# Weight sums by DMA, last state columns split, and two zeroed banks for lags in an S5 mixer kernel

## The chip, the cores and the metric

The kernel runs on one core of a Trainium2 chip. The core has five engines that work side by side, each on its own queue of instructions in order: PE (TensorE, matmuls; its weight loads are shown as PEld), DVE (VectorE), ACT (ScalarE), POOL (GpSimd) and SP (SyncE, here used for DMA). They meet through semaphores: an instruction waits until a semaphore has a count, and whatever stands behind it on the same engine waits too. Times are device microseconds (us), smaller is better.

## What is computed

One layer of a diffusion backbone over 1024 latent tokens of width 1024, with a prefix of 256 context tokens. The layer is an S5 mixer (a bidirectional state space model with complex diagonal states, 64 groups of 16 channels and 64 states) with GELU and a gate (GLU), then a SwiGLU FFN, each behind an RMSNorm with shift, scale and gate. Cut to what matters here:

```python
def s5_direction(u_ctx, u_lat, lam_re, lam_im, log_step, b_re, b_im, c_re, c_im):
    lam_bar = jnp.exp(lam * jnp.exp(log_step)[:, None])
    b_bar = ((lam_bar - 1.0) / lam)[..., None] * lax.complex(b_re, b_im)
    def run(u, h0):
        bu = jnp.einsum('lgh,gnh->lgn', u, b_bar)
        bu = bu.at[0].add(lam_bar * h0)
        _, h = lax.associative_scan(_linear_combine, (a, bu), axis=0)
        return jnp.einsum('lgn,ghn->lgh', h, c_mat).real, h[-1]
...
x = x + m_l[2][:, None] * y_l
h_l = modulate(rms_norm(x, norm_ffn[i]), m_l[3][:, None], m_l[4][:, None])
x = x + m_l[5][:, None] * swiglu(h_l, ffn_w1[i], ffn_w3[i], ffn_w2[i])
return rms_norm(x, norm_final)
```

## The kernel before

Eight tokens are taken as one chunk, so the latent stream is 128 chunks. Inside a chunk the output comes from a lag matrix (what the 8 tokens of the chunk give to each other) and from the state at the chunk's border. The 64 groups are handled as 8 units `k` of 8 groups; a quarter `q` holds two units.

Up to some 129 us the kernel loads, builds powers of lambda, projects the tokens into the states and runs the context. Then three things stand beside each other:

- `scan()` on DVE: the recurrence over the latent chunks. At each step it makes two products in `st1` and `st2`, which are the columns 384 to 512 of two PSUM banks, `LTb` (`ltb` in the profile) and `ltc`, and adds them to the states. For two of the quarters it fills all columns itself; for the others it goes in steps of two, and POOL restores the columns between. `scan()` is recorded ahead of the order string below, so its instructions are known to the program when the string's are added.
- `PROG1`, an order string written by hand: each word is an operation that is recorded at its place on all engines that it uses.
- After it the PSUM pools of this stage are closed, and `PROG2`, a second order string, follows: the late halves, the gelu, the transposes and the GLU. Then come the gates and the FFN.

The words that matter: `A` ada matmuls (modulation) with their weight loads on SP. `B0` turns the input matrices on PE and copies them on ACT. `Cqp` builds part p of the weights CL of quarter q: two products on POOL (`prod`), the second into a buffer `ct`, and their sum, whose way is a letter of `HOWS`: P is on PE (matmuls with an identity into a bank, L672, and ACT copies, L673), E is an add on POOL (L77), Y is a DMA issued by POOL that accumulates (L675). `Gq` is a sign change of the loaded C matrices on ACT (L655), which `Lq` loads. `Kn` computes lag rows (`k_mats`, PE L809 to L817), from two PSUM tiles that ACT zeroes ahead (L771), copies them on ACT (L821) and stores them to HBM (L822). `Tn` loads them back as lag matrices (SP, L830). `F` restores columns of the scan on POOL. `Rk`, `Zk`, `zk` copy the states in turned order for the backward direction (L902 on ACT, L904 elsewhere). `Pk` is the lag matmuls (`x_mm`, L945) and the early states (L922) of unit k into banks of the stage's PSUM pool, `Yn` ACT's copy of them out (L993). `Nk` is the late states, `Dk` their add on DVE, `Hk` the gelu. `Qk` is lag matmuls and all states in one (L935), only for units 6 and 7. `M0` and `M1` make modulation columns.

A PSUM pool of this stage has three banks `pw` in turn, and one `pm`. A helper `tt` records every two-operand op, so these have line 77. In the profile `c` stands for a weight tile, `ra`, `rw`, `rxa`, `rxc`, `ru` for regions of SBUF.

Of the kernel before, what the change touches and what calls it, by code (L numbers as in the profile page):

```python
# [17 lines left out]
P = 128  # L18
# [5 lines left out]
T = 8  # L24
G = 64
HC = 16
NS = 64
EPS = 1e-6
MAGIC = 12582912.0
HOWS = "PPPP PPEE PEEE EEEE"  # L30
ZEN = "VVSVSVSV"
PROG1 = ("A22 B0 A26 C02 G1 A30 A34 C03 A40 K0 A44 A48 C10 K1 L2 A54 G2 C11 A60 F10 C12 F11 C13 T0 T1 T2 T3 A64 M0 M1 K2 R0 P0 Y0 Y1 K3 L3 R1 C20 P1 Y2 Y3 T4 T5 G3 T6 T7 C21 C22 C23 K4 R2 P2 Y4 Y5 K5 R3 P3 Y6 Y7 T8 T9 T10 T11 C30 C31 R4 P4 Y8 Y9 C32 C33 R5 P5 Y10 Y11 K7 K6 M2 m0 F30 F31")
PROG2 = ("T12 T13 T14 T15 Z0 N0 Z1 Z2 D0 Z3 N1 D1 Z4 H0 H1 N2 D2 H2 w0 w1 l1 N3 Z5 D3 H3 N4 D4 z6 z7 I0 J0 I1 J1 H4 N5 D5 I2 J2 H5 I3 J3 W0 W1 x0 x1 x2 x3"
         " Q6 H6 I4 J4 Q7 b0 I5 J5 H7 g03 g13 I6 J6 g23 g05 g15 I7 J7 V1 w20 w21 g26 x10 x11 x12 x13")
LOG2E = 1.4426950408889634
LN2H = 0.693359375
LN2L = -2.12194440e-4
# [5 lines left out]
def s5_ffn_kernel(tc, a, out):  # L43
# [3 lines left out]
    with ctx:  # L47
# [611 lines left out]
        def cl_ops(q, part, ct, how):  # L659
# [7 lines left out]
            def add():  # L667
# [8 lines left out]
                else:  # L676
# [14 lines left out]
                 7: [(1, [0], 0, 8)], 8: [(1, [0], 8, 16)], 9: [(1, [1, 2, 3])],  # L691
                 11: [(2, [0], 0, 8)], 12: [(2, [0], 8, 16)], 13: [(2, [1, 2, 3])],
                 14: [(3, range(4), 0, 8)]}
        ct_ = [view(r, kb, [8, T, HC]) for r, kb in ((RW, 0), (RC[3], 0), (RC[3], 4), (RA, STB))]
        cts = [[ct_[0], ct_[0], ct_[1], ct_[2]], [ct_[0], ct_[1], ct_[2], ct_[0]], [ct_[1], ct_[2], ct_[0], ct_[1]], [ct_[3], ct_[0]] * 2]
        CL0 = cl_ops(0, 0, cts[0][0], SY) + cl_ops(0, 1, cts[0][1], SY)
        CLAT = {12: 1, 13: 1, 14: 2}
        for hb in range(16):
# [164 lines left out]
            while rest:  # L863
                one()

        def fill(q, h, reg, kb):

            tmps = [view(reg, kb + i, [256]) for i in range(2)]
            st, c0 = STQ[q], 32 * h
            for e in (0, 8):  # L870
                rot(st[:, 32 + c0:63 + c0:2, :, e:e + 8], st[:, 31 + c0:62 + c0:2, :, e:e + 8], LS[:, 0], 16 * q + e, E, tmps)

        MBd = dr.tile([2, 2, 512], F32, tag="mbd", name="mbd")

# [34 lines left out]
        def yview(k, gp):  # L909
            return Y[:, k].rearrange("p t (a e h) -> p e a t h", e=2, h=HC)[:, gp]  # L910

        def states_mm(k, pts, half, hs, start):

            for a_ in range(4):
                for ri in range(2):
                    for d in range(2):
                        cs_ = slice(64 * (half ^ d), 64 * (half ^ d) + 64)
                        c0 = 31 + 64 * half
                        for gp in range(2):
                            ps = slice(64 * gp, 64 * gp + 64)  # L920
                            st = hs[ps, :, ri, a_] if d else STQ[k // 2][ps, c0:c0 + 64, ri, 8 * (k % 2) + a_]
                            PE.matmul(flat(pts[gp][cs_, a_]), st, flat(CL[k // 2][ps, ri, d, 4 * (k % 2) + a_]),  # L922
                                      start=start and ri == 0, stop=ri == 1 and (start or a_ == 3))

        def states_all(k, pts, hs):

            for a_ in range(4):
                for ri in range(2):
                    for d in range(2):
                        for c in range(2):  # L930
                            cs_ = slice(64 * c, 64 * c + 64)
                            for gp in range(2):
                                ps = slice(64 * gp, 64 * gp + 64)
                                st = hs[ps, cs_, ri, a_] if d else STQ[k // 2][ps, 31 + 64 * c:95 + 64 * c, ri, 8 * (k % 2) + a_]
                                PE.matmul(flat(pts[gp][cs_, a_]), st, flat(CL[k // 2][ps, ri, d, 4 * (k % 2) + a_]),  # L935
                                          start=False, stop=a_ + ri + d == 5)

        def x_mm(k, pool):

            pts = [pool([4, T, HC]) for _ in range(2)]  # L940
# [5 lines left out]
            return pts  # L946

        scan()
        inner = {}
        HSe = [view(r, kb, [64, 2, 4]) for r, kb in ((RC[3], 14), (RC[3], 12), (RC[3], 14), (RC[3], 12), (RA, 2), (RA, 0))]  # L950
        HSl = [view(RA, STB * (i // 3) + 4.125 + 2 * (i % 3), [64, 2, 4]) for i in range(6)]
        HSq = {6: view(RA, 0, [P, 2, 4]), 7: view(RA, STB, [P, 2, 4])}

        def run(prog):


            for w in prog.split():
                op, i = w[0], int(w[1:])
                if op == "A":
                    ada(i)  # L960
                elif op == "M":
                    mod_cols(i)
                elif op == "K":
                    k_mats(*divmod(i, 2), [zeros(pw([15 * HC])) if i == 6 else kt, zeros(pw([15 * HC])) if i in (0, 1, 2, 3, 6) else pm[:, 0:15 * HC]])
                elif op == "L":
                    cs_load(i, S)
                elif op == "G":
                    cs_sign(i)
                elif op == "B":
                    bb_put(1, bb_turn(1))  # L970
                    bb_put(0, bb_turn(0))
                elif op == "C":
                    q, part = divmod(i, 10)
                    for f in cl_ops(q, part, cts[q][part], HOW[q][part]):
                        f()
                elif op == "F":
                    fill(*divmod(i, 10), *((RW, 0) if i >= 30 else (RC[3], 12)))
                elif op == "T":
                    toeplitz(i)
                elif op == "R":  # L980
                    turned(i, 0, HSe[i], S)
                elif op == "Z":
                    turned(i, 1, HSl[i], ENG[ZEN[i]])
                elif op == "z":
                    turned(i, 2, HSq[i], ENG[ZEN[i]])
                elif op == "P":
                    inner[i] = x_mm(i, pw)
                    states_mm(i, inner[i], 0, HSe[i], False)
                elif op == "Q":
                    inner[i] = x_mm(i, pe8)  # L990
                    states_all(i, inner[i], HSq[i])
                elif op == "Y":
                    S.copy(yview(i // 2, i % 2), inner[i // 2][i % 2])  # L993
                elif op == "N":
                    late[i] = [pe8([4, T, HC]) for _ in range(2)]
                    states_mm(i, late[i], 1, HSl[i], True)
                elif op == "D":
                    for gp, po in enumerate(late[i]):
                        tt(yview(i, gp), po, yview(i, gp), ADD)
                elif op == "H":  # L1000
                    if i in late:
                        S.activation(Y[:, i], Y[:, i], AF.Gelu_apprx_tanh)
                    else:
                        for gp in range(2):
                            S.activation(yview(i, gp), inner[i][gp], AF.Gelu_apprx_tanh)
                elif op == "I":
                    if GH[0] is None:
                        GH[0] = tuple(view(region(t, 16, R32), 0, [4, 8, P]) for t in ("c1", "c0"))
                    late[i] = gt_hi(i, 0)
                elif op == "J":  # L1010
                    gt_lo(i, 0, late[i])
                elif op == "W":
                    if not WR:
                        W0.append(region("c2", 16, R32))
                        WR.append((view(W0[0], 0, [8 * 256]), view(W0[0], 8, [8 * 256])))
                    v = slice(1024 * i, 1024 * i + 1024)
                    split(wr0[i], (WR[0][0][:, v], WR[0][1][:, v]), E, V)
                elif op == "w":
                    cq, h = divmod(i, 10)
                    SY.dma_start(wr0[h], a["w_glu"][cq][:, 1024 * h:1024 * h + 1024])  # L1020
                elif op == "b":
                    SY.dma_start(bglu, a["b_glu"].to_broadcast([P, D]))
                elif op == "l":
                    load_glu(i)
                elif op == "m":
                    mod_row(0)
                elif op == "x":
                    gate(i % 10, slice(4 * (i // 10), 4 * (i // 10) + 4))
                elif op == "V":
                    GR.append(region("ra", 80.5, R32))  # L1030
                    GH[1] = (view(GR[0], 0, [4, 8, P]), view(GR[0], 16, [4, 8, P]))
                    WR.extend((view(GR[0], kb, [8 * 256]), view(GR[0], kb + 8, [8 * 256])) for kb in (32, 48, 64))
                    split(wraw, WR[i], E)
                elif op == "g":
                    glu_mm(0, i // 10, range(i % 10 + 1))
# [732 lines left out]
```

## Time and profile before

| | |
|---|---|
| time, median of 3 runs | 1016.01 us (1014.42 to 1016.13) |
| the profiled execution | 1015.21 us |
| its span in the trace | 1013.4 us |
| mean granted PE clock | 0.992 |
| PE in the scan, 129.5 to 229.5 us | 84.97 of 100 us busy |
| DVE there | 97.81 of 100 us busy |

The span is what the trace covers; the execution's own time is 1.8 us longer. The busy rows of the page show PE at 95% of the span, so over the whole kernel it is PE that sets the time; but the shares are means over stages, and the stage of the scan has to be read by itself. In a row of the timeline stand the start, the duration, the engine, the line, the operation with out<-in by the program's names, the shape, and in brackets the idle time of that engine just before, with what ended it.

### The profile page before, as it was taken

How to read it: one execution, taken by the hardware profiler on the slowest of the kernel's cores; microseconds unless marked ns; L12 is line 12 of the kernel's file. 1: busy time of each engine (PE TensorE's matmuls, PEld its weight loads, DVE VectorE, ACT ScalarE, POOL GpSimd, SP SyncE). 2: the span in 40 equal slices, each digit the busy share in tenths (PEclk: the TensorE clock that was granted, in tenths of full speed). 3: DMA queues.
4: the chain of work that ended last, by engine and by line, in shares of the span. 5: the costliest groups of instructions: out<-in, count | busy, mean ns of one | idle time of the engine just before them, and what ended most of it. 6: DMA issues, size and time to landing. Idle time of an engine off the chain costs nothing. (4 is left out here: it accounts for less than half of the span.)

```text
span 1013.4 us, 18560 instructions
## 1 busy us (share of the span) xinstructions
PE 959.4 (95%) x6988; PEld 772.1 (76%) x6988; DVE 780.4 (77%) x1638; ACT 438.9 (43%) x860; POOL 763.4 (75%) x590
## 2 busy tenths in 40 slices
PE   5988798779999999999999999999999999999996
PEld 1466523679999988778888888888888888888885
DVE  7989699996356867877958677686959677686987
ACT  5478622335444663443343343324343343324337
POOL 5799998994672448979785878777786878777764
PEclk9999999999999999999999999999999999999998
DMA  9765997334512021011212111121212111121205
GB/s 336 280 135 95 280 346 247 95 84 138 188 46 80 2 104 63 27 44 46 73 42 83 42 52 42 50 66 53 73 42 83 43 52 43 46 70 53 73 22 166
DMA packets 48546, 98.96 MB, mean 98 GB/s; under 512 B 4284, under 2 KB 18876, under 8 KB 47176
## 3 DMA queue, kind: packets, MB, share of 16 engines
q1 hardware_dynamic: 43272, 86.64, 26.0%
q0 software_dynamic: 2016, 7.34, 3.9%
q10 hardware_dynamic: 3168, 3.79, 1.1%
q8 instruction: 55, 0.90, 0.4%
q14 instruction: 35, 0.29, 0.1%
HBM read 84.25 MB, written 6.17 MB: 89 GB/s over the span
## 5 line engine op out<-in xcount | busy, mean ns | idle before, releaser
L77 POOL TENSOR_TENSOR c<-rxc,c 128x512 fp32r<-128x512 f32 x128 | 166.6, 1315 | 53.5 <-ACT c L1222 52.7
L1282 PE MATMUL ut<-ra,c 128*128 128x512 f32 x400 | 155.7, 389 | 1.2 <-DVE ra L77 1.2
L1281 PE MATMUL ut<-ra,c 128*128 128x512 f32 x400 | 155.7, 389 | 0.2 <-ACT ra L1222 0.2
L1283 PE MATMUL ut<-ra,c 128*128 128x512 f32 x400 | 155.6, 389 | 0.0
L1222 ACT CAST c<-rxc 128x512 fp32r<-128x512 f32 x128 | 79.1, 622 | 147.0 <-PE xt L1576 53.3
L1576 PE MATMUL xt<-c,c 128*128 128x512 f32 x540 | 129.7, 389 | 0.0
L1576 PEld LDWEIGHTS xt<-c,c 128*128 128x128 f32 x540 | 101.4, 188 | 21.0
L77 DVE TENSOR_TENSOR ru<-ru,xt 128x1024 f32<-128x1024 f32 x90 | 107.3, 1215 | 10.9 <-PE xt L1576 7.9
L77 DVE TENSOR_TENSOR ru<-ut,ru 128x512 f32<-128x512 f32 x98 | 67.2, 686 | 43.0 <-PE ut L1283 37.6
L1282 PEld LDWEIGHTS ut<-ra,c 128*128 128x128 f32 x400 | 75.1, 188 | 17.0 <-POOL rxc L77 1.5
L1281 PEld LDWEIGHTS ut<-ra,c 128*128 128x128 f32 x400 | 75.1, 188 | 16.1 <-ACT ra L1222 0.6
L1283 PEld LDWEIGHTS ut<-ra,c 128*128 128x128 f32 x400 | 75.1, 188 | 15.5
L77 POOL TENSOR_TENSOR c<-rw,c 128x512 fp32r<-128x512 f32 (+1 forms) x29 | 41.1, 1417 | 37.8 <-ACT c L1222 37.8
L77 POOL TENSOR_TENSOR c<-ru,c 128x512 fp32r<-128x512 f32 (+1 forms) x39 | 57.1, 1465 | 10.1 <-ACT c L1222 5.7
L1281 PE MATMUL ut<-c,c 128*128 128x512 f32 x160 | 62.3, 390 | 0.8 <-DVE rxa L77 0.8
L77 POOL TENSOR_TENSOR rxc<-rxc 128x512 f32<-128x512 f32 x40 | 61.4, 1535 | 1.6
L1282 PE MATMUL ut<-c,c 128*128 128x512 f32 x160 | 62.2, 389 | 0.0
L1283 PE MATMUL ut<-c,c 128*128 128x512 f32 x160 | 62.2, 389 | 0.0
L1576 PE MATMUL ut<-c,c 128*128 128x512 f32 x216 | 51.9, 389 | 0.0
L584 PE MATMUL pv<-ru,c 128*64 128x160 f32 x512 | 45.0, 316 | 5.6 <-ACT rxa L388 1.8
L77 DVE TENSOR_TENSOR pe<-pe,ru 128x256 f32<-128x256 f32 x64 | 27.4, 429 | 29.5 <-ACT pe L1122 17.4
L77 DVE TENSOR_TENSOR ru<-ru,ut 128x512 f32<-128x512 f32 x76 | 47.3, 680 | 0.3
(444 smaller groups left out, 2569.1 us busy)
## 6 DMA issues: line engine op xcount, KB each, us to landing
c<-in_ada_w SPq DMA_DIRECT2D x46, 256.0 KB
rxc<-in_w SPq DMA_DIRECT2D x38, 256.0 KB
rxc<-in_w SPq DMA_DIRECT2D x19, 512.0 KB
ru<-in_w SPq DMA_DIRECT2D x11, 512.0 KB
rw<-in_w SPq DMA_DIRECT2D x11, 512.0 KB
ra<-in_ada_w SPq DMA_DIRECT2D x10, 512.0 KB
ra<-in_ada_w SPq DMA_DIRECT2D x18, 256.0 KB
ru<-in_xT SPq DMA_DIRECT2D x4, 1024.0 KB
```

The costliest lines, as they stand in the source:

```text
L77: eng.tensor_tensor(out=o, in0=x, in1=y, op=op)
L584: PE.matmul(pv[64 * (i % 2):64 * (i % 2) + 64, ri, c0:c0 + 160], w[:, i, 64 * ri:64 * ri + 64], U[:, 8 * b + 4 * j + i], start=True, stop= ...
L1222: S.copy(o[0], x)
L1281: PE.matmul(pu, wh, bh, start=start, stop=False)
L1282: PE.matmul(pu, wh, bl, start=False, stop=False)
L1283: PE.matmul(pu, wl, bh, start=False, stop=stop)
L1576: PE.matmul(pd, w[:, cs_], b, start=j in (1, 2, 4) and n == 0, stop=n == 2, skip_group_check=j not in (1, 2, 4))
```

## The change

It does three things. Five of the weight sums (C21, C22, C30, C31, C32) go from an add on POOL to an accumulating DMA, with two more operand buffers (`ct_[3]`, `ct_[4]`), and the sum of C33 goes to PE. The columns of the last quarter are restored by unit (`F6`, `F7`, 8 ops of 512) in place of by half (`F30`, `F31`, 16 ops of 256); the early states of units 6 and 7 are computed in the first string (`P6`, `P7`, with `Y12` to `Y15`), and `Q6`, `Q7` become `N6`, `N7` with adds `D6`, `D7`. And a new op `O0` behind `B0` zeroes the columns 0 to 240 of `LTb` and `ltc` on ACT, for the lags of K5 and K7; K4 moves behind P2, and K6, K7 behind C33.

```diff
--- before.py
+++ after.py
@@ -27,11 +27,11 @@
 NS = 64
 EPS = 1e-6
 MAGIC = 12582912.0
-HOWS = "PPPP PPEE PEEE EEEE"
+HOWS = "PPPP PPEE PYYE YYYP"
 ZEN = "VVSVSVSV"
-PROG1 = ("A22 B0 A26 C02 G1 A30 A34 C03 A40 K0 A44 A48 C10 K1 L2 A54 G2 C11 A60 F10 C12 F11 C13 T0 T1 T2 T3 A64 M0 M1 K2 R0 P0 Y0 Y1 K3 L3 R1 C20 P1 Y2 Y3 T4 T5 G3 T6 T7 C21 C22 C23 K4 R2 P2 Y4 Y5 K5 R3 P3 Y6 Y7 T8 T9 T10 T11 C30 C31 R4 P4 Y8 Y9 C32 C33 R5 P5 Y10 Y11 K7 K6 M2 m0 F30 F31")
-PROG2 = ("T12 T13 T14 T15 Z0 N0 Z1 Z2 D0 Z3 N1 D1 Z4 H0 H1 N2 D2 H2 w0 w1 l1 N3 Z5 D3 H3 N4 D4 z6 z7 I0 J0 I1 J1 H4 N5 D5 I2 J2 H5 I3 J3 W0 W1 x0 x1 x2 x3"
-         " Q6 H6 I4 J4 Q7 b0 I5 J5 H7 g03 g13 I6 J6 g23 g05 g15 I7 J7 V1 w20 w21 g26 x10 x11 x12 x13")
+PROG1 = ("A22 B0 O0 A26 C02 G1 A30 A34 C03 A40 K0 A44 A48 C10 K1 L2 A54 G2 C11 A60 F10 C12 F11 C13 T0 T1 T2 T3 A64 M0 M1 K2 R0 P0 Y0 Y1 K3 L3 R1 C20 P1 Y2 Y3 T4 T5 G3 T6 T7 C21 C22 C23 R2 P2 Y4 Y5 K4 K5 R3 P3 Y6 Y7 T8 T9 T10 T11 C30 C31 R4 P4 Y8 Y9 C32 R5 P5 Y10 Y11 C33 K6 K7 M2 m0 F6 R6 P6 Y12 Y13 F7 R7 P7 Y14 Y15")
+PROG2 = ("T12 T13 T14 T15 Z0 N0 Z1 Z2 D0 Z3 N1 D1 Z4 H0 H1 N2 D2 H2 w0 w1 l1 Z6 N3 Z5 D3 H3 Z7 N4 D4 I0 J0 I1 J1 H4 N5 D5 I2 J2 H5 I3 J3 W0 W1 x0 x1 x2 x3"
+         " N6 D6 H6 I4 J4 N7 D7 b0 I5 J5 H7 g03 g13 I6 J6 g23 g05 g15 I7 J7 V1 w20 w21 g26 x10 x11 x12 x13")
 LOG2E = 1.4426950408889634
 LN2H = 0.693359375
 LN2L = -2.12194440e-4
@@ -691,8 +691,8 @@
                  7: [(1, [0], 0, 8)], 8: [(1, [0], 8, 16)], 9: [(1, [1, 2, 3])],
                  11: [(2, [0], 0, 8)], 12: [(2, [0], 8, 16)], 13: [(2, [1, 2, 3])],
                  14: [(3, range(4), 0, 8)]}
-        ct_ = [view(r, kb, [8, T, HC]) for r, kb in ((RW, 0), (RC[3], 0), (RC[3], 4), (RA, STB))]
-        cts = [[ct_[0], ct_[0], ct_[1], ct_[2]], [ct_[0], ct_[1], ct_[2], ct_[0]], [ct_[1], ct_[2], ct_[0], ct_[1]], [ct_[3], ct_[0]] * 2]
+        ct_ = [view(r, kb, [8, T, HC]) for r, kb in ((RW, 0), (RC[3], 0), (RC[3], 4), (RA, STB), (RA, STB + 4.125))]
+        cts = [[ct_[0], ct_[0], ct_[1], ct_[2]], [ct_[0], ct_[1], ct_[2], ct_[0]], [ct_[1], ct_[3], ct_[0], ct_[2]], [ct_[3], ct_[0], ct_[4], ct_[3]]]
         CL0 = cl_ops(0, 0, cts[0][0], SY) + cl_ops(0, 1, cts[0][1], SY)
         CLAT = {12: 1, 13: 1, 14: 2}
         for hb in range(16):
@@ -863,12 +863,18 @@
             while rest:
                 one()
 
-        def fill(q, h, reg, kb):
-
-            tmps = [view(reg, kb + i, [256]) for i in range(2)]
+        def fill_q(q, h):
+
+            tmps = [view(RC[3], 12 + i, [256]) for i in range(2)]
             st, c0 = STQ[q], 32 * h
             for e in (0, 8):
                 rot(st[:, 32 + c0:63 + c0:2, :, e:e + 8], st[:, 31 + c0:62 + c0:2, :, e:e + 8], LS[:, 0], 16 * q + e, E, tmps)
+
+        def fill_k(k):
+
+            tmps = [view(RA, 4.25 + 2 * i, [512]) for i in range(2)]
+            st, e = STQ[k // 2], 8 * (k % 2)
+            rot(st[:, 32:95:2, :, e:e + 8], st[:, 31:94:2, :, e:e + 8], LS[:, 0], 8 * k, E, tmps)
 
         MBd = dr.tile([2, 2, 512], F32, tag="mbd", name="mbd")
 
@@ -909,6 +915,9 @@
         def yview(k, gp):
             return Y[:, k].rearrange("p t (a e h) -> p e a t h", e=2, h=HC)[:, gp]
 
+        def ypart(k, gp):
+            return view(RA, 2 * STB + 4.25 + 2 * gp, [4, T, HC]) if k == 7 else yview(k, gp)
+
         def states_mm(k, pts, half, hs, start):
 
             for a_ in range(4):
@@ -922,19 +931,6 @@
                             PE.matmul(flat(pts[gp][cs_, a_]), st, flat(CL[k // 2][ps, ri, d, 4 * (k % 2) + a_]),
                                       start=start and ri == 0, stop=ri == 1 and (start or a_ == 3))
 
-        def states_all(k, pts, hs):
-
-            for a_ in range(4):
-                for ri in range(2):
-                    for d in range(2):
-                        for c in range(2):
-                            cs_ = slice(64 * c, 64 * c + 64)
-                            for gp in range(2):
-                                ps = slice(64 * gp, 64 * gp + 64)
-                                st = hs[ps, cs_, ri, a_] if d else STQ[k // 2][ps, 31 + 64 * c:95 + 64 * c, ri, 8 * (k % 2) + a_]
-                                PE.matmul(flat(pts[gp][cs_, a_]), st, flat(CL[k // 2][ps, ri, d, 4 * (k % 2) + a_]),
-                                          start=False, stop=a_ + ri + d == 5)
-
         def x_mm(k, pool):
 
             pts = [pool([4, T, HC]) for _ in range(2)]
@@ -946,10 +942,9 @@
             return pts
 
         scan()
-        inner = {}
-        HSe = [view(r, kb, [64, 2, 4]) for r, kb in ((RC[3], 14), (RC[3], 12), (RC[3], 14), (RC[3], 12), (RA, 2), (RA, 0))]
-        HSl = [view(RA, STB * (i // 3) + 4.125 + 2 * (i % 3), [64, 2, 4]) for i in range(6)]
-        HSq = {6: view(RA, 0, [P, 2, 4]), 7: view(RA, STB, [P, 2, 4])}
+        inner, KO = {}, []
+        HSe = [view(r, kb, [64, 2, 4]) for r, kb in ((RC[3], 14), (RC[3], 12), (RC[3], 14), (RC[3], 12), (RA, 2), (RA, 0), (RA, 2), (RA, 0))]
+        HSl = [view(RA, STB * (i // 4) + 4 + 2 * (i % 4), [64, 2, 4]) for i in range(8)]
 
         def run(prog):
 
@@ -958,10 +953,12 @@
                 op, i = w[0], int(w[1:])
                 if op == "A":
                     ada(i)
+                elif op == "O":
+                    KO.extend(zeros(t[:, 0:15 * HC]) for t in (LTb, ltc))
                 elif op == "M":
                     mod_cols(i)
                 elif op == "K":
-                    k_mats(*divmod(i, 2), [zeros(pw([15 * HC])) if i == 6 else kt, zeros(pw([15 * HC])) if i in (0, 1, 2, 3, 6) else pm[:, 0:15 * HC]])
+                    k_mats(*divmod(i, 2), [kt, zeros(pw([15 * HC])) if i < 4 else pm[:, 0:15 * HC]] if i % 2 == 0 or i < 4 else KO)
                 elif op == "L":
                     cs_load(i, S)
                 elif op == "G":
@@ -974,35 +971,29 @@
                     for f in cl_ops(q, part, cts[q][part], HOW[q][part]):
                         f()
                 elif op == "F":
-                    fill(*divmod(i, 10), *((RW, 0) if i >= 30 else (RC[3], 12)))
+                    if i < 10:
+                        fill_k(i)
+                    else:
+                        fill_q(*divmod(i, 10))
                 elif op == "T":
                     toeplitz(i)
                 elif op == "R":
                     turned(i, 0, HSe[i], S)
                 elif op == "Z":
                     turned(i, 1, HSl[i], ENG[ZEN[i]])
-                elif op == "z":
-                    turned(i, 2, HSq[i], ENG[ZEN[i]])
                 elif op == "P":
-                    inner[i] = x_mm(i, pw)
-                    states_mm(i, inner[i], 0, HSe[i], False)
-                elif op == "Q":
-                    inner[i] = x_mm(i, pe8)
-                    states_all(i, inner[i], HSq[i])
+                    inner[i] = x_mm(i, pw) if i < 6 else [pw([4, T, HC]) for _ in range(2)]
+                    states_mm(i, inner[i], 0, HSe[i], i >= 6)
                 elif op == "Y":
-                    S.copy(yview(i // 2, i % 2), inner[i // 2][i % 2])
+                    S.copy(ypart(i // 2, i % 2), inner[i // 2][i % 2])
                 elif op == "N":
-                    late[i] = [pe8([4, T, HC]) for _ in range(2)]
-                    states_mm(i, late[i], 1, HSl[i], True)
+                    late[i] = [pe8([4, T, HC]) for _ in range(2)] if i < 6 else x_mm(i, pe8)
+                    states_mm(i, late[i], 1, HSl[i], i < 6)
                 elif op == "D":
                     for gp, po in enumerate(late[i]):
-                        tt(yview(i, gp), po, yview(i, gp), ADD)
+                        tt(yview(i, gp), po, ypart(i, gp), ADD)
                 elif op == "H":
-                    if i in late:
-                        S.activation(Y[:, i], Y[:, i], AF.Gelu_apprx_tanh)
-                    else:
-                        for gp in range(2):
-                            S.activation(yview(i, gp), inner[i][gp], AF.Gelu_apprx_tanh)
+                    S.activation(Y[:, i], Y[:, i], AF.Gelu_apprx_tanh)
                 elif op == "I":
                     if GH[0] is None:
                         GH[0] = tuple(view(region(t, 16, R32), 0, [4, 8, P]) for t in ("c1", "c0"))
```

On ACT, at the start of the scan, this is what moves: the end of `B0` (`L797`), the two new zero copies, then the copies of C02's sum (`L673`) and the sign change of `G1` (`L655`).

```order
 L797 COPY c_66<-pw 128x512 x2
+L771 COPY ltb<-r_60 128x240
+L771 COPY ltc<-r_60 128x240
 L673 COPY c_63<-pw 128x512 x2
 L655 ACTIVATE rxc<-rxc 128x768
```

The same place of the changed kernel, with the semaphores that each row waits for (PE_49 is PE's, DVE_49 is DVE's):

```order
L797 COPY c_66<-pw 128x512 [waits PE_49]
L797 COPY c_66<-pw 128x512
L771 COPY ltb<-r_60 128x240 [waits DVE_49]
L771 COPY ltc<-r_60 128x240 [waits DVE_49]
L673 COPY c_63<-pw 128x512 [waits DMAHW3_49,PE_49]
L673 COPY c_63<-pw 128x512 [waits DMAHW4_49,PE_49]
L655 ACTIVATE rxc<-rxc 128x768 [waits DMAHW2_49]
```

Two copies now stand between B0 and C02, and each waits for DVE. In the built program the counts that they wait for are 823 and 824, which DVE reaches with the last two adds of `scan()`.

On ACT, at the end of the first string, before: the copies of units 4 and 5 (`L993`) with their turned copies (`L902`), the lags of K7 from `kt` and `pm`, the zeroing of two `pw` banks, and the lags of K6 from them.

```order
L902 COPY ra<-ra 128x512
L993 COPY ru<-pw 128x4x8x16 x2
L821 COPY rw<-kt 128x240
L822 DMA kd_1249<-rw 128x240
L821 COPY rw<-pm 128x240
L822 DMA kd_1249<-rw 128x240
L771 COPY pw<-r_60 128x240 x2
L821 COPY r_60<-pw 128x240
L822 DMA kd_1249<-r_60 128x240
```

The same place in the changed kernel (L908 is the turned copy, L988 the copy out):

```order
L988 COPY ru<-pw 128x4x8x16 x2
L673 COPY c_66<-pw 128x512 x2
L821 COPY r_60<-kt 128x240
L822 DMA kd_1249<-r_60 128x240
...
L821 COPY rw<-ltc 128x240
L822 DMA kd_1249<-rw 128x240
L908 COPY ra<-ra 128x512
L988 COPY ru<-pw 128x4x8x16 x2
L908 COPY ra<-ra 128x512
L988 COPY ra<-pw 128x512 x2
```

C33's sum now stands ahead of the lags of K6 and K7, which come from `kt`, `pm`, `ltb` and `ltc` with no zeroing between, and the turned copies and the copies out of units 6 and 7 follow them.

## Prediction

> **What bounds the kernel now.** I read the page first, then the busy time by windows around the stretch that the change touches.
>
> ```profile
> span 1013.4 us, 18560 instructions
> PE 959.4 (95%) x6988; PEld 772.1 (76%) x6988; DVE 780.4 (77%) x1638; ACT 438.9 (43%) x860; POOL 763.4 (75%) x590
> ...
> 129.50:229.50 100.00, 84.97 (x1788) 49.97 (x1780) 97.81 (x509) 27.94 (x60) 95.69 (x66) 0.98 0.57 185
> 250.00:272.00 22.00, 22.00 (x328) 21.64 (x321) 4.81 (x9) 8.90 (x15) 12.61 (x7) 1.00 0.52 169
> ```
>
> The last two rows are windows: stretch and length, then busy time of PE, PEld, DVE, ACT and POOL, the granted clock, the DMA share and GB/s. Over the whole span PE is the bound. It is not in the 100 us from 129.5: there DVE is busy 97.81 us with the scan, and PE, ACT and POOL do the work of the first order string beside it. From 250 on PE has no gap (22.00 of 22.00), so what is taken from or added to PE there counts in full. Two things set the time, then: when the late state matmuls (N0) may start, and how much PE has after them.
>
> The timeline of DVE, then of ACT, shows the ends of the scan and what stands around the place of O0, the added op (start, duration, instruction, and in brackets the idle time before it and its releaser):
>
> ```profile
> 129.57 0.29 DVE L77 TENSOR_TENSOR ltb<-ra,lta 128x128 f32<-128x128 f32 x1
> 228.82 0.28 DVE L77 TENSOR_TENSOR ra<-ltb,ra 128x128 f32<-128x128 f32 x1
> 229.14 0.29 DVE L77 TENSOR_TENSOR ra<-ltc,ra 128x128 f32<-128x128 f32 x1
> ...
> 134.34 1.07 ACT L797 COPY c<-pw 128x512 f32<-128x512 f32 x2 [0.69 <-PE pw L791]
> 138.34 0.58 ACT L673 COPY c<-pw 128x512 f32<-128x512 f32 x1 [2.93 <-PE pw L672]
> 140.54 0.85 ACT L655 ACTIVATE rxc<-rxc 128x768 f32<-128x768 f32 x1
> ```
>
> The scan writes a product into each of the banks ltb and ltc at every step, from 129.57, and its last two adds read them at 228.82 and 229.14; the last ends at 229.43. ACT's B0 ends at 135.4, and C02's first copy stands next at 138.34.
>
> **O0, the large term.** O0 puts two ACT copies of zeros into ltb[:,0:240] and ltc[:,0:240] right behind B0. The scan uses columns 384 to 512 of the same two tiles, and it is recorded ahead of the string. In the built program each of the copies waits for a count of DVE's semaphore (823 and 824), and the instructions that raise it to these are the last two adds of the scan: the tile is what is ordered, not its columns. So O0 doesn't run at 135.4 but at 229.1, and all behind it on ACT's queue waits too. Nothing in the scan waits for O0, so the scan goes on to its end and there is no deadlock.
>
> Behind O0 stand C02's two copies, which free the banks that PE fills next, and the sign op of L655, whose result POOL multiplies. These rows show where POOL and PE stop:
>
> ```profile
> 141.46 2.10 POOL L77 TENSOR_TENSOR rw<-rxc,rxa 128x1024 f32<-128x1024 f32 x1
> 162.26 1.40 POOL L77 TENSOR_TENSOR c<-ra,r 128x256 f32<-128x256 f32 x2 [2.67 <-DVE ra L77]
> 172.03 2.34 POOL L77 TENSOR_TENSOR c<-c,rw 128x1024 f32<-128x1024 f32 x1
> ...
> 143.88 3.70 PE L672 MATMUL pw<-c,r 128*128 128x512 f32 x8
> 169.08 2.36 PE L531 MATMUL pm<-c,r 128*2 128x512 f32 x6 [1.90 <-DMA c<-in_ada_w]
> 175.88 0.27 PE L809 MATMUL pw<-c,c 64*16 64x112 f32 x1 [0.32 <-ACT pw L771]
> ```
>
> ACT restarts: the zeros take 0.36 us each as copies of that shape do (225.33 below), the second from 229.43 to 229.79, so C02's first copy stands at 229.80 in place of 138.34. **PE** has three banks in turn; the second half of C03 (143.88 + 1.85 = 145.73) needs that of C02's first copy, now free at 229.80 + 0.58 = 230.38: +84.65. **POOL** needs the sign op: 229.80 + 1.07 (two copies) + 0.85 = 231.72 in place of 141.46: +90.26. Its later wait of 2.67 us on the scan goes, since the scan is over: +87.6.
>
> Where the two meet is K2 (175.88), which needs the last weight sum of the second quarter from POOL (172.03 + 2.34 = 174.37, now 262.0). PE would be there at 175.88 + 84.65 = 260.5, less the wait of 1.90 for a weight load that now has 84 us to arrive, plus some lost clock, as in this row of another, shorter gap:
>
> ```profile
> 199.20:202.60 3.40, 3.40 (x16) 3.20 (x16) 3.33 (x19) 1.29 (x3) 3.32 (x3) 0.50 0.26 83
> ```
>
> The clock was 0.50 for 3.40 us there, so some 1.7 us of work is lost: 260.3. POOL is later, and K2 stands at 262.0: **+86.1** for everything behind it.
>
> The Trainium skill, "PSUM — Partial Sum Buffer", section "PSUM bank collisions raise a hardware error", speaks against this edit: it says that two engines on one bank and quadrant at once raise an error and spoil data even at disjoint columns, and that banks are to be guarded whole. By it the wait can't be spared while the scan has these banks; by columns alone there would be no wait, and the sum would lack its 86.1. No row here shows two engines in one bank at once, which agrees so far as it goes.
>
> **The moved work, up to N0.** I give times on the clock of before, to which 86.1 is added at the end. P1 ends at 194.06 in both. These rows carry the walk:
>
> ```profile
> 197.60 0.27 PE L809 MATMUL kt<-c,rxa 64*16 64x112 f32 x1 [3.14 <-POOL c L77]
> 213.77 1.13 PE L945 MATMUL pw<-ra,ru 128*128 128x128 f32 x8 [2.77 <-DMA ra<-kd]
> 215.61 1.16 PE L945 MATMUL pw<-ra,ru 128*128 128x128 f32 x8 [0.71 <-DMA ra<-kd]
> 229.58 0.69 PE L922 MATMUL pe<-c,ra 64*64 64x128 f32 x4 [0.31 <-DVE ra L77]
> 230.62 0.64 PE L922 MATMUL pe<-c,ra 64*64 64x128 f32 x12 [0.35 <-DVE ra L904]
> ...
> 186.69 1.72 ACTq L822 DMA_DIRECT2D kd<-rw  x1
> 199.15 0.36 ACT L821 COPY r<-kt 128x240 f32<-128x240 f32 x1 [3.18 <-PE pm L817]
> 207.71 0.33 ACTq L822 DMA_DIRECT2D kd<-rw  x1
> 225.33 0.36 ACT L821 COPY rw<-kt 128x240 f32<-128x240 f32 x1 [0.57 <-PE pm L817]
> 226.53 0.33 ACTq L822 DMA_DIRECT2D kd<-rw  x1
> 208.08 0.62 ACT L902 COPY c<-ra 128x512 f32<-128x512 f32 x1 [0.40 <-ACT rw L821]
> 223.69 1.07 ACT L993 COPY ru<-pw 128x512 f32<-128x512 f32 x2 [3.11 <-PE pw L922]
> ...
> L922 PE MATMUL pw<-c,c 64*64 64x128 f32 x32 | 2.3, 290 | 0.0
> L672 PE MATMUL pw<-c,r 128*128 128x512 f32 x8 | 3.7, 605 | 0.0
> L935 PE MATMUL pe<-c,ra 64*64 64x128 f32 x128 | 4.3, 287 | 0.0
> ```
>
> Columns of the last three: busy us and mean ns, of PE's groups in a window each. P2 no longer stands behind K4's wait of 3.14 us for POOL. It waits for its lag matrices: the last store of a pair is issued at 208.04 (207.71 + 0.33), and the two halves of P4 start 5.7 and 7.5 us later (213.77, 215.61). The stores for P2 end at 188.4, so its halves stand at 194.1 and 195.9, the second ends at 197.0, and early states (2.3) end it at 199.3. K4 took 1.6 (197.60 to the copy at 199.15), so K4 and K5 end at 202.5, P3 (2.1 + 2.3) at 206.9. K5's copies and stores take 1.5 (225.33 to 226.86): 204.0, which is 4.0 earlier than 208.04. P4's second half starts at 211.5 and ends with its states at 215.0, P5 (4.4) at 219.4. Now comes what is new on PE here: C33's sum, 3.7 to 223.1 with its last copy to 223.7; K6 and K7, 3.2 to 226.9; their copies and stores on ACT to 228.4; then in a row of waits between ACT and PE: turned copy R6 0.62, P6's 64 matmuls 2.3, two copies Y12 and Y13 1.07, R7 0.62, P7 2.3, which ends at 235.3. N0 follows, against 230.6 before: **+4.7**. Of this C33's 8 matmuls, P6 and P7 are 8.3 us of PE, of which 4 were bought by K4's lost wait.
>
> **Behind N0.** Q6 and Q7 held 128 state matmuls each (4.3); N6 and N7 hold 64 (2.3). The x matmuls are the same 16. PE has no gap here: 2 x (4.3 - 2.3) = **-4.0**. The adds D6 and D7 go to DVE (4.81 of 22 busy) and the gelu ops turn from two to one on ACT (8.90 of 22): cover enough, at nothing; without it some 2 us.
>
> **POOL's own edits.**
>
> ```profile
> L77 POOL TENSOR_TENSOR c<-c,rw 128x1024 f32<-128x1024 f32 x4 | 9.5, 2367 | 0.3
> L77 POOL TENSOR_TENSOR c<-rxc,rxa 128x1024 f32<-128x1024 f32 x18 | 36.5, 2063 | 0.1
> L77 POOL TENSOR_TENSOR rw<-ra,r 128x256 f32<-128x256 f32 x8 | 5.8, 750 | 0.0
> ...
> L675 POOL DMA_DIRECT2D c<-rw x2: 862/869/876, 119.8 to 130.8; - x2
> DMA to landing us min/median/max: 7.0/7.8/8.6
> ...
> 220.95 2.38 POOL L77 TENSOR_TENSOR c<-c,rw 128x1024 f32<-128x1024 f32 x1
> ```
>
> Six adds of 2.37 go; five issues of 0.87 come, so POOL ends C33's products 5 x 1.50 before 220.9, at 213.4, and with its shift at 301.0. PE wants them at 219.4 + 86.1 = 305.5: hidden by 4.5. The sums land after at most 8.6 us: C22's before K4 with about 1 us to spare, C32's before K6 with more; without cover up to 8.6 - 2.4 = 6 us. The own operand buffers make no product wait for a sum in flight. The restoring falls from 16 ops of 256 columns (0.75) to 8 of 512, which no row shows; by the bounds 0.75 and 2.06 I take 1.2, so 9.6 us, to 310.6. R6 wants its half at 228.4 + 86.1 = 314.5: hidden, and at 2.06 each it would be late by some 2 us at R7's half alone.
>
> **The sum**: 86.1 + 4.7 - 4.0 = +86.8. The profiled execution is 1015.2 us (span 1013.4), which gives 1102.0; the median of before, 1016.0, lies 0.8 higher, so **1103** (1102.8) for the median.
>
> **The rivals.**
> - *No stall*: O0's copies wait only for what used the banks ahead of the scan, at 129.6, and run at 135.4. For it: the columns are disjoint. Against it: the count in the built program. Then N0 stands at 235.3 by the walk, +4.7 - 4.0 = 1016.7; if the row of ACT and PE steps ends under the scan (N0 can't stand before 230.6), -4.0 = 1012.0, the faster side. It decides at the start of ltb's zeros: ahead of 136 us or behind 229. Chance 0.05.
> - *POOL sets the pace after the restart, and PE's row is shorter than I walked*: N0 can't stand before POOL's last restoring (310.6) with R7 and P7 (2.9) behind it, at 313.5 against my 321.4: 1103 - 7.9 = 1095. For it: POOL restarts last. Against it: DMA trips of 5.7 and 7.5 us that no faster POOL shortens. Chance 0.08.
> - *ACT's shift of 91.5 carries through* (229.80 - 138.34) in place of 86.1, as each pair of copies has its turn on ACT: 1016.0 + 91.5 + 4.7 - 4.0 = 1108.2, and 1.1 more where N0's bank waits for Y14 and Y15. Against it: ACT is busy 27.94 of 100 and can catch up. Chance 0.10.
>
> **How the numbers follow.** The forecast has 0.77. The range of 8 in 10 goes from near the POOL rival to above the ACT rival, 1096 to 1111, and leaves out the first. Runs of this kernel spread 1.7 us, so 0.2% (2 us) is what can be told from no change. Faster by that 0.02, within 0.03 (both from the first rival), slower 0.95.
>
> **What would show it.** ACT's zero copy of ltb starts near 229.1 with some 94 us idle and DVE as releaser; the first window has ACT, PE and POOL idle for most of 136 to 229; the scan's last add still ends near 229.4; PE's C03 second half stands at 230.4, POOL's product into rw at 231.7, K2 at 262, N0 at 321; the span is near 1100. I am wrong if ltb's zeros start before 136, if the scan's end moves, or if N0 minus K2 is not near 59 us.

## The result and the profile after

The changed kernel takes **1115.39 us** (1113.42 to 1117.13, 4 runs) against 1016.07 us (1014.42 to 1016.73, 4 runs) before: ratio 1.098, 95% interval [1.0954, 1.1005], 99.3 us more. The forecast was 1103 in a range of 1096 to 1111: the direction and the large term held, the size did not, by 12 us. The profiled execution has a span of 1114.8 us, 101.4 more than before.

The page after, then the busy time by windows (as before: stretch, length, PE, PEld, DVE, ACT, POOL, clock, DMA share, GB/s):

```profile
span 1114.8 us, 18589 instructions
PE 969.8 (87%) x6996; PEld 778.1 (70%) x6996; DVE 781.5 (70%) x1642; ACT 442.6 (40%) x866; POOL 752.2 (67%) x581
...
129.50:229.50 100.00, 15.65 (x60) 3.81 (x58) 96.79 (x504) 3.60 (x8) 11.40 (x7) 0.61 0.20 70
278.00:335.00 57.00, 41.93 (x1036) 35.91 (x1038) 0.86 (x2) 14.51 (x29) 32.66 (x24) 0.79 0.44 111
350.00:372.00 22.00, 22.00 (x283) 21.41 (x278) 9.84 (x16) 10.40 (x13) 12.53 (x7) 1.00 0.53 169
```

In the 100 us of the scan PE falls from 84.97 to 15.65 us busy and ACT from 27.94 to 3.60, while DVE keeps its pace: the other engines stand. In the window behind N0 (the last row) PE is as gapless as it was. The row between covers P1's end to N0: 57 us in which PE is busy 41.93 and the granted clock is 0.79. From P1's end to N0 before, where C33's sum, P6 and P7 (forecast at 8.3 us of PE) did not yet stand, it was this row:

```profile
194.00:231.00 37.00, 27.43 (x916) 24.97 (x916) 35.05 (x152) 12.02 (x26) 36.29 (x27) 0.95 0.32 91
```

The timelines of ACT, POOL and PE of the changed kernel at the places that the prediction named:

```profile
228.05 0.36 ACT L771 COPY ltb<-r 128x240 f32<-128x240 f32 x1 [91.63 <-DVE ra L77]
228.37 0.36 ACT L771 COPY ltc<-r 128x240 f32<-128x240 f32 x1
228.67 1.06 ACT L673 COPY c<-pw 128x512 f32<-128x512 f32 x2
...
230.56 2.01 POOL L77 TENSOR_TENSOR rw<-rxc,rxa 128x1024 f32<-128x1024 f32 x1 [89.36 <-ACT rxc L655]
...
229.30 2.93 PE L672 MATMUL pw<-c,r 128*128 128x512 f32 x3 [83.74 <-ACT c L673]
260.71 0.27 PE L809 MATMUL kt<-c,c 64*16 64x112 f32 x1 [0.46 <-POOL c L77]
281.78 1.62 PE L941 MATMUL pw<-ra,ru 128*128 128x128 f32 x6 [3.66 <-DMA ra<-kd]
293.08 0.25 PE L809 MATMUL ltc<-c,rxa 64*16 64x112 f32 x1 [2.22 <-issue]
303.35 1.13 PE L941 MATMUL pw<-ra,ru 128*128 128x128 f32 x8 [3.66 <-DMA ra<-kd]
305.37 1.01 PE L941 MATMUL pw<-ra,ru 128*128 128x128 f32 x3 [0.89 <-DMA ra<-kd]
334.73 0.49 PE L931 MATMUL pe<-c,ra 64*64 64x128 f32 x2
```

The first five show the stall as forecast: the zeros wait 91.63 us for DVE, then POOL 89.36 for the sign op and PE 83.74 for ACT's copy. The rest show what was not forecast: PE waits 3.66 us for the lag loads of P2 and as long for those of P4, stands 2.22 us in the middle of K5 for nothing that the profile shows, and comes to N0 at 334.7 where 321.4 was forecast. From N0 to the end of the span it is 780.1 us, and was 783.8.

### The profile page after: what moved, and what is told of

Same layout as the page of the kernel before. It is cut to its first block, busy times and chain, and to the rows that moved or that the text cites. A ratio compares the mean times of both kernels' runs of the same rounds, so it can differ in the third digit from the quotient of the medians.

```text
span 1114.8 us, 18589 instructions
## 1 busy us (share of the span) xinstructions
PE 969.8 (87%) x6996; PEld 778.1 (70%) x6996; DVE 781.5 (70%) x1642; ACT 442.6 (40%) x866; POOL 752.2 (67%) x581
## 5 line engine op out<-in xcount | busy, mean ns | idle before, releaser
L1567 PEld LDWEIGHTS xt<-c,c 128*128 128x128 f32 x540 | 101.4, 188 | 21.0
L672 PE MATMUL pw<-c,r 128*128 128x512 f32 x40 | 21.0, 655 | 83.7 <-ACT c L673 83.7
L77 POOL TENSOR_TENSOR rw<-rxc,rxa 128x1024 f32<-128x1024 f32 x6 | 12.7, 2116 | 91.5 <-ACT rxc L655 89.4
L672 PEld LDWEIGHTS pw<-c,r 128*128 128x128 f32 x40 | 7.5, 203 | 95.0 <-ACT c L673 84.6
L77 POOL TENSOR_TENSOR c<-rw,c 128x512 fp32r<-128x512 f32 (+1 forms) x29 | 41.2, 1420 | 37.8 <-ACT c L1213 37.8
L1272 PE MATMUL ut<-c,c 128*128 128x512 f32 x160 | 62.3, 390 | 0.8 <-DVE rxa L77 0.8
L1274 PE MATMUL ut<-c,c 128*128 128x512 f32 x160 | 62.3, 389 | 0.0
L1273 PE MATMUL ut<-c,c 128*128 128x512 f32 x160 | 62.2, 389 | 0.0
```

The source lines that it names most:

```text
L77: eng.tensor_tensor(out=o, in0=x, in1=y, op=op)
L672: PE.matmul(pc, ident, src[:, hs].rearrange("p g t h -> p (g t h)"), start=i == 0, stop=i == 1)
L1272: PE.matmul(pu, wh, bh, start=start, stop=False)
L1273: PE.matmul(pu, wh, bl, start=False, stop=False)
L1274: PE.matmul(pu, wl, bh, start=False, stop=stop)
L1567: PE.matmul(pd, w[:, cs_], b, start=j in (1, 2, 4) and n == 0, stop=n == 2, skip_group_check=j not in (1, 2, 4))
```

## The experiments

Each edit is against the changed kernel or the kernel before, as said, and is cut to its main lines. Times stand beside the median of before in the same series.

**1. The zeros alone, in the kernel before.**

```diff
-PROG1 = ("A22 B0 A26 ...
+PROG1 = ("A22 B0 O0 A26 ...
+                elif op == "O":
+                    for t in (LTb, ltc):
+                        zeros(t[:, 0:15 * HC])
```

> The kernel before with only the two zero copies of O0 behind B0; nothing reads them. Theory A (the zeros wait for the scan's end and hold ACT, then PE and POOL): K2 moves by some 84 us as in the changed kernel, and with the rest of the old program behind it the time is 1097 to 1103 us. Rival (the stall comes from the new buffers or sums, not from the zeros): 1016 us as before, zeros at about 135 us.

Measured: 1103.53 against 1017.49, ratio 1.0853 [1.0828, 1.0879], +86.0. Two copies of 0.36 us that nobody reads cost 86 us, as theory A had it (0.5 us above its range). K2 itself moved by 83.9 us, from 175.88 to 259.82; the rest came behind it, where K4's wait for POOL grew from 3.14 to 5.56. Its ACT row:

```profile
227.36 0.36 ACT L771 COPY ltb<-r 128x240 f32<-128x240 f32 x1 [90.79 <-DVE ra L77]
```

**2 to 4. The zeros taken out, the sums taken back, both.**

```diff
-PROG1 = ("A22 B0 O0 A26 ...
+PROG1 = ("A22 B0 A26 ...
-... if i % 2 == 0 or i < 4 else KO)
+... if i % 2 == 0 or i < 4 else [zeros(pw([15 * HC])) for _ in range(2)])
```
```diff
-HOWS = "PPPP PPEE PYYE YYYP"
+HOWS = "PPPP PPEE PEEE EEEP"
```

> The changed kernel without O0; the lags of K5 and K7 go to banks of the stage's pool that ACT zeroes, as those of K6 did before. Theory A: ACT doesn't stop, and what is left over 1016 is the price of the rest of the change, 1115.4 less 84 to 85: 1026 to 1033 us. Rival (my walk on record, the moved work costs +4.7 and gives 4.0 back): 1016 to 1018 us. Rival (the stall isn't from O0): still 1110 or more.

> The changed kernel, zeros kept, with the five weight sums back as adds on POOL (C33 stays on PE). Theory A (the sums' transfers lengthen the trip of the lag rows to HBM and back): the waits of P2 (3.7 us) and P4 (3.7 and 0.9) for lag loads shrink by 4 to 8 us in all, time 1105 to 1110 us. Theory B (the new order and the slowed clock behind each gap make the excess, the sums do nothing): 1114 to 1119 us, since POOL is 1.5 us later for each add.

> Both undone: no zeros of O0, five sums as adds on POOL; what is left of the change is the order of K4, K6, K7, the split of units 6 and 7, the restoring by unit and C33's sum on PE. Theory A: below the kernel without zeros by 4 to 8 us, 1019 to 1026 us. Theory B: equal to the kernel without zeros, 1026 to 1033 us. My walk on record: 1016 to 1019 us.

| kernel | us | ratio to before (1017.49) |
|---|---|---|
| without the zeros | 1032.79 | 1.0156 [1.0124, 1.0189] |
| sums on POOL | 1110.60 | 1.0916 [1.0887, 1.0946] |
| both | 1028.23 | 1.0105 [1.0076, 1.0135] |

So the zeros are worth 82.6 us in the changed kernel (1115.39 - 1032.79, from two series), and the rest of the change is itself 15.3 us slower, which my walk gave at +0.7. The five sums are worth 4.8 us with the stall (1115.39 - 1110.60, from two series) and 4.6 without it (within one series). The lag loads of P2, without the zeros, first with the sums by DMA, then with the adds:

```profile
196.13 1.13 PE L941 MATMUL pw<-ra,ru 128*128 128x128 f32 x8 [3.35 <-DMA ra<-kd]
...
195.05 2.54 PE L941 MATMUL pw<-ra,ru 128*128 128x128 f32 x16 [0.35 <-DMA ra<-kd]
```

The wait falls from 3.35 to 0.35 us. With the zeros kept it falls from 3.66 to 1.06, and P4's from 3.66 to 2.84. The sums and the lag rows are in flight together (in the changed kernel C22's sum from 274.1 to 279.8, P2's rows from 272.1 to 281.8) and the trips get longer. 10.7 us are left with both undone: 4.6 below the kernel without zeros, as theory A had the difference, but above its range, since that kernel itself came out at the top of its own.

**5 to 7. Each other part alone, in the kernel before.** The split of units 6 and 7 with its restoring, the second order string of the changed kernel and its operand buffers; the sums with their buffers (C33 stays on POOL); the order of K4, K6 and K7.

```diff
-... C32 C33 R5 P5 Y10 Y11 K7 K6 M2 m0 F30 F31
+... C32 C33 R5 P5 Y10 Y11 K7 K6 M2 m0 F6 R6 P6 Y12 Y13 F7 R7 P7 Y14 Y15
```
```diff
-HOWS = "PPPP PPEE PEEE EEEE"
+HOWS = "PPPP PPEE PYYE YYYE"
```
```diff
-... C23 K4 R2 P2 Y4 Y5 K5 ... C32 C33 R5 P5 Y10 Y11 K7 K6
+... C23 R2 P2 Y4 Y5 K4 K5 ... C32 R5 P5 Y10 Y11 C33 K6 K7
```

> The kernel before with one part of the change alone: units 6 and 7 split in early and late halves, their columns restored by unit (F6, F7). No zeros, sums as before, lags in the order of before. Theory S (of the 10.7 us that are left without zeros and without DMA sums, most is the row of steps R6, P6, Y12, Y13, R7, P7 that now stands between the last lags and N0): N0 6 to 10 us later, 4.0 given back behind it, 1019 to 1023 us. Theory O (most is the new order of the lags): 1014 to 1018 us.

> The kernel before with the five weight sums by DMA and their buffers alone; C33's sum stays an add on POOL. Theory T (traffic of the sums lengthens the trip of the lag rows): the waits of P2 and P4 for lag loads grow by 2 to 4 us each, and the time is 1017 to 1022 us although POOL is relieved of 7.5 us. Rival (the relief of POOL wins, K4's wait of 3.1 us goes): 1012 to 1016 us.

> The kernel before with the new order of the lags alone (K4 behind P2, C33 ahead of K6, K7), zeros for K5 and K7 in banks of the pool. Theory O: 1020 to 1026 us, since K5 waits 2 us for its zeros and P4's loads come later. Theory S: 1015 to 1018 us, since K4's wait of 3.1 us goes in exchange.

| kernel | us | ratio to before (1017.36) |
|---|---|---|
| split alone | 1021.43 | 1.0033 [1.0014, 1.0053] |
| sums alone | 1019.59 | 1.0030 [1.0009, 1.0050] |
| order alone | 1018.56 | 1.0022 [1.0002, 1.0043] |

Each part is slower by itself, by the ratios some 3.4, 3.1 and 2.2 us (by the medians 4.1, 2.2 and 1.2); the third is hardly clear of the noise. The first is nearly as theory S had it (N0 6 to 10 us later): with the split N0 stands at 235.5 in place of 229.6, 5.9 later, and some 4 come back behind it. The second has the time of theory T and half of its mechanism: P2, which had no wait for lag loads before, waits 1.39 and 2.49 us for them, but P4's two waits grew only from 3.5 to 4.3 us together. The third lies between its two cases. By the ratios they make 8.7 of the 15.3 us together; C33 on PE and what the parts do to each other hold the rest, and were not taken apart further.

**8. The last lags behind P6 and P7**, without the zeros.

```diff
-... C33 K6 K7 M2 m0 F6 R6 P6 Y12 Y13 F7 R7 P7 Y14 Y15
+... C33 M2 m0 F6 R6 P6 K6 Y12 Y13 F7 R7 P7 Y14 Y15 K7
```

> The changed kernel without the zeros (1032.8 us), with K6 and K7 put behind P6 and P7, so that the lags of the last quarter, wanted only by N6 and N7 30 us later, no longer stand ahead of the early halves. Theory S: the steps of ACT and PE overlap with the lags, 3 to 6 us less, 1027 to 1030 us. Rival (the chain is not these steps but PE's sum of work): 1031 to 1034 us.

Measured: 1034.32, ratio 1.0167 [1.0127, 1.0206]: nothing won, a miss. N0 stands at 248.6 against 246.7: K7 now waits for banks that Y14 and Y15 free, and N0 for K7's copies. The rival has it.

**9 and 10. A filler for the clock.** `X` is a number of extra matmuls into columns of `pm` that nobody reads then; they are there to keep PE busy in its waits.

```diff
+                elif op == "X":
+                    for _ in range(i):
+                        PE.matmul(pm[:, 256:512], ident, CL[0][:, 0, 0].rearrange("p g t h -> p (g t h)")[:, 0:256], start=True, stop=True)
-... R2 P2 ... R4 P4 ... R6 P6 ...
+... R2 X12 P2 ... R4 X12 P4 ... R6 X6 P6 ...
```

> The changed kernel, zeros and sums kept, with matmuls that do nothing useful in three of PE's waits: 12 of 128x256 ahead of P2, 12 ahead of P4, 6 ahead of P6, into columns of the bank pm that nobody reads then. Theory H (the granted clock falls to 0.5 behind each gap of 3 us, and the moved matmuls of P2, P3, P4, P6, P7 run at it, 8 to 9 us in all): the clock stays at 1.0 behind the filled gaps, P2's lag matmuls take 2.1 us in place of 3.75, P4's second half 1.2 in place of 2.1, time 1108 to 1112 us. Rival (transfers and ACT set the pace there, so a faster PE only waits longer): 1114 to 1118 us.

> The same filler with the five sums as adds on POOL (1110.6 us without the filler). Theory H: 1103 to 1107 us, near what was forecast on record. Rival: 1109 to 1113 us.

Measured: 1117.17, ratio 1.0961 [1.0933, 1.0988], and 1113.84, ratio 1.0931 [1.0907, 1.0956]. The first lies in the rival's range, the second above both ranges. My own sizing was at fault: 12 such matmuls took 5.45 us in a gap of 3.66, so P2's lag matmuls ran at full clock (1.95 us) but started later. The two runs don't tell what the clock is worth.

**11 and 12. K4 at its old place, and the zeros ahead of the scan.**

```diff
-... C23 R2 P2 Y4 Y5 K4 K5 ...
+... C23 K4 R2 P2 Y4 Y5 K5 ...
```
```diff
-PROG1 = ("A22 B0 O0 A26 ...
+PROG1 = ("A22 B0 A26 ...
+        KO = [zeros(t[:, 0:15 * HC]) for t in (LTb, ltc)]
         scan()
-                elif op == "O":
-                    KO.extend(zeros(t[:, 0:15 * HC]) for t in (LTb, ltc))
```

> The changed kernel with K4 back ahead of P2, so that K4 and K5 don't stand back to back. In the changed kernel PE stands still for 2.2 us in the middle of K5, with no releaser that the profile shows, and 1.5 us in K7 behind K6. Theory B (the gap comes from two lag ops back to back, over 500 PE instructions in 3 us): the gap in K5 goes, that in K7 stays; time 1112 to 1116 us, since K4 waits for POOL again. Rival (the gap comes with the writes into the banks ltb and ltc): it stays, 1115 to 1119 us.

> The changed kernel with the two zero copies recorded ahead of the scan, so that they don't wait for it. Theory A (a bank is guarded whole, whatever the columns): ACT goes on at 130, but now K5's first matmuls into ltb and ltc wait for the scan's last adds, so PE stands from some 203 to 228 or 229; N0 near 273, time 1050 to 1060 us. Rival (the place of the zeros alone was at fault): no wait of K5, 1029 to 1034 us as without the zeros.

Measured for K4: 1115.62, ratio 1.0936 [1.0895, 1.0977], no difference that can be told. But with K4 and K5 apart K5 has no gap of its own, and K7 behind K6 keeps one of 1.8 us: theory B. Measured for the zeros: 1050.95, ratio 1.0319 [1.0291, 1.0348], as theory A had it. First its zeros on ACT, then PE's first matmul into ltb:

```profile
127.87 0.35 ACT L771 COPY ltb<-r 128x240 f32<-128x240 f32 x1
...
227.93 0.55 PE L809 MATMUL ltb<-c,rxa 64*16 64x112 f32 x2 [24.72 <-DVE ra L77]
```

The zeros run at once, and the wait for the scan turns up at K5 instead, 24.72 us long. It is the whole tile that is held until the scan's end, not a place in ACT's queue. Each of the two tiles is one bank, so these runs don't tell whether the order goes by tile or by bank.

**13 and 14. A filler that ends inside the gaps.**

```diff
-... R2 P2 ... R4 P4 ...
+... R2 X7 P2 ... R4 X7 P4 ...
```

In the second, with the sums on POOL, `R4 X6 P4` alone.

> The changed kernel with a filler that ends inside the gaps: 7 matmuls of 128x256 (some 3.2 us by the first filler's 5.45 for 12) ahead of P2 and 7 ahead of P4, each of which waits 3.66 us for its lag loads, none elsewhere. Theory H (the slowed clock behind the gaps is part of what N0 is late): P2 ends some 2.3 us earlier against its own start, P4 2.4, of which 2 to 4 us reach N0: 1111 to 1113.5 us beside 1115.4. Rival (ACT, the stores and their loads set the pace, a warm PE waits in the next place): 1114.5 to 1117 us.

> The changed kernel with the five sums as adds on POOL (1110.6 us) and 6 such matmuls ahead of P4 alone, whose gap there is 2.85 us. Theory H: P4's second half and its states take 3.5 us in place of 5.8, and 1108 to 1109.5 us. Rival: 1110 to 1112 us.

Measured: 1118.32, ratio 1.0999 [1.0975, 1.1023], and 1108.74, ratio 1.0904 [1.0879, 1.0928]. In the first the clock held and P2 ended at 285.5 in place of 288.4, but the gap in K5 grew. The second is in theory H's range and 1.9 below its pair without filler, from two series; by the ratios it is 1.2, and the intervals overlap. In the two profiled executions its N0 stands 3.1 us earlier (326.7 against 329.8). Gap in K5 of the first:

```profile
291.89 0.25 PE L809 MATMUL ltb<-c,rxa 64*16 64x112 f32 x1 [3.62 <-issue]
```

So of 2.9 us won in P2, 1.4 went into a longer wait in K5, and the clock was low again behind it. P4 ended 3.5 us earlier than in the changed kernel (307.6 against 311.1), but K7 no earlier (325.2 against 324.8), since its gap without a releaser, 1.47 us there, became two of 1.38 and 2.19 us. The rival has the sign, not the reason: PE did wait in the next place, but for no transfer of lag rows, and the time lies 1.3 us above the rival's range. A PE at full clock alone doesn't make the excess go.

## Why the prediction went as it did

- **The wait of O0 was right.** Zeros at 228.1 (forecast 229.1), C03's second half at 229.3 (230.4), POOL's product at 230.6 (231.7), K2's wait for POOL ends at 260.7 (262.0). All four are 1.0 to 1.3 us early because the scan itself started 1.1 us earlier in this execution (128.47 against 129.57) and ended at 228.3 and not at 229.4. Runs 1 and 2 show the stall from both sides, at 86.0 and 82.6 us for a forecast of 86.1; run 12 shows that the whole tile is held, on which it rests. That run 1 agrees to 0.1 us is in part luck: K2 itself moved by 83.9 us there and by 84.8 in the changed kernel.
- **One term in it failed**: I let PE's wait for a weight load go, as it had 84 us to arrive. It is still there, 1.8 us. SP's loads need buffers that PE's own matmuls free, so they stood still with PE (SP's longest wait for PE's L531 was 88.2 us). POOL hid the error, since K2 waits for POOL.
- **The step that failed is "the moved work, up to N0", +4.7.** Between P1 and N0 the work took 56.6 us (278.1 to 334.7) where my walk had 41.2, 15.4 more. By the prediction's own sign of being wrong, N0 minus K2 was 74.0 us and not near 59. One us more comes from a slip: the walk's +4.7 counts from 230.6, where N0 goes on after its second wait, but N0's first matmul stood at 229.58; read the same way as in the changed kernel, the walk gives +5.7. The steps in order:

| end of | forecast | measured |
|---|---|---|
| P1 | 280.2 | 278.1 |
| P2 | 285.4 | 288.4 |
| K5 | 288.6 | 294.0 |
| P3 | 293.0 | 299.7 |
| P4 | 301.1 | 311.1 |
| P5 | 305.5 | 315.8 |
| K7 | 313.0 | 324.8 |
| P7, N0 starts | 321.4 | 334.7 |

  Three things were missing in it. *The sums' transfers*: I asked only whether they land in time ("hidden"), not what they do to other transfers. P2's first half started 9.7 us behind the last store's issue and P4's halves 7.9 and 9.9, where I took 5.7 and 7.5 from before; with the adds in their place (run 3) these are 6.8, 6.4 and 8.5. The sums are some 5 us of the excess, shown by runs 3 and 4. The last store and the first matmul of P2, in the changed kernel and (second row; there the last store was issued by 272.17) with the adds:

```profile
271.22 0.89 ACTq L822 DMA_DIRECT2D kd<-rw  x1
...
278.95 1.13 PE L941 MATMUL pw<-ra,ru 128*128 128x128 f32 x8 [1.06 <-DMA ra<-kd]
```

  *The clock*: I took full-clock durations for matmuls that stand behind gaps, though I had quoted a stretch behind such a gap at 0.50. P2's lag matmuls took 3.75 us for 2.05, at this clock:

```profile
282.00:286.00 4.00, 4.00 (x28) 3.78 (x32) 0.00 (x0) 0.00 (x0) 3.70 (x3) 0.50 0.48 141
```

  Added up over P2, P3, P4, P6 and P7, the matmuls took some 9 us longer than at full clock, my estimate from these rows and those of before; it overlaps with the other two terms, since it is their gaps that the slow clock stands behind. What the clock is worth by itself stays open: run 14 hints at 1 to 3 us, run 13 won nothing. *The gaps in K5 and K7*, 2.2 and 1.5 us. No row of before shows such a gap, since there the only two lag ops in a row, K7 and K6, had a wait of 2.04 us for zeroed banks between them; run 11 ties them to lag ops back to back.
- **Behind N0, -4.0 was right in size**: 783.8 to 780.1 is -3.7. Some of that is luck: it holds a new gap of 1.51 us at 341.25, again without a releaser, that the forecast did not have, and two gaps of 0.35 and 0.34 us of before are gone.
- **POOL's relief was right and worth nothing**, as forecast: POOL ended F7 at 317.8 and R7 copied it at 331.0. A wait that I had not seen (5.95 us before C32's second product, until PE had read P3's states) stayed under that cover.
- **The rivals**: the one without a stall is refuted; POOL didn't set the pace. ACT's later shift gave about the size, 1108 to 1109, by a mechanism that did not occur: PE waited for the lag loads, and K5 stood for no releaser. 1115.4 lies above them all: the range ended just above the ACT rival and left nothing for transfers in each other's way, slowed matmuls and gaps without a releaser.

No version here beats the kernel before. The part that gives something back (the split, some 4 us behind N0) puts a row of ACT and PE steps ahead of N0: with the split alone N0 is 5.9 us later.

## What to carry to other kernels

Free columns of a bank are not a free bank: before putting anything there, look for who is the last to use that bank in recorded order, and what stands behind the new instruction on its own queue; two copies of 0.36 us held three engines for 84 to 92 us here. When work leaves an engine for a DMA, ask not only whether the DMA lands in time but which round trips through memory are in flight with it. When a walk moves matmuls behind gaps, take their durations from rows behind such gaps. And a wait that is taken away may come back under another name: in run 2 K5 and K7 waited 2.0 us each for zeroed banks; in the changed kernel, without that wait, they stood still for 2.2 and 1.5 us.

## What was not expected of the hardware

PE's gaps of over 1 us without a releaser ("issue") ended 1.2 to 1.6 us after a transfer of 16 KB on the instruction queue: so for all three of the changed kernel, and for all 28 in the traces of these runs. The kernel before has none. In the changed kernel the one in K5 runs from 290.9 to 293.1; this is the row of DMA queues for the window 290.7 to 291.8, and the window 287 to 290.7 ahead of it has none (queue, packets, MB, share of 16 engines):

```profile
q8 instruction: 1, 0.02, 5.4%
```

In run 13 the transfer ran from 289.3 to 290.3 and the gap ended at 291.9. So PE seems to run out of instructions. A lag op is 289 of them on PE, weight loads included, and by 290.9 PE had run over 400 in the 2.5 us since K4 began. Back-to-back lag ops are one such place, the small state matmuls around N0 another (341.25). In run 13, finishing the work ahead sooner only made the gap longer. That it is the instructions which PE waits for is inferred from these times; a shorter instruction stream was not tried.

The way of a pair of lag rows to HBM and back as a matrix, from the last store's issue to P2's first matmul, took 9.7 us in the changed kernel with weight sums of 512 KB in flight and 6.8 in run 3, which differs only in having these sums as adds on POOL.

The clock did not go by the length of the gap alone. It was 0.50 behind the gap of 2.22 us in K5 (294.2 to 297.5 in the changed kernel), and 1.00 behind one of 2.77 us in the kernel before (P4's lag matmuls at 213.77).
